# Who makes the low parts of block 2's weights: 42 subtractions move from the vector engine to GpSimd

## The chip, the cores and the metric

The kernel runs on one core of one Trainium2 chip. The metric is the device time of one execution in microseconds (us). The engines are named as the profile names them: PE (TensorE, matmuls), DVE (VectorE), ACT (ScalarE), POOL (GpSimd) and SP (the queue that issues most DMAs). SBUF is the memory on which all engines work, PSUM the small one into which PE writes.

## The reference

Two transformer blocks of two layers each run over 512 tokens of width 1024, all in float32. The change lies in the mixer of block 2, which is called once a layer, so twice in an execution:

```python
def hybrid_mixer(h, positions, w_in, ...):
    (cq, k_att, v_att, k_idx, w_idx,
     q_m, k_m, v_m, o_m, i_m, f_m) = jnp.split(h @ w_in, split_pts, axis=-1)
    cq = rms_norm_2(cq, q_latent_norm)
    q = rope((cq @ w_q_up)...); q_idx = rope((cq @ w_qidx_up)...); k = rope(k_att...)
    att = dsa_attention(q, k, v, q_idx, k_idx, w_idx)      # 256 keys a query, chosen by an indexer
    qk = jax.nn.silu(causal_dwconv(jnp.concatenate([q_m, k_m], -1), conv_w, conv_b))
    hm = mlstm_chunkwise(...)                              # four heads of 128
    hm = jax.nn.sigmoid(o_m) * rms_norm_2(hm, mlstm_out_norm)
    return jnp.concatenate([att, hm], axis=-1) @ w_out
```

The indexer takes relu(q_idx k_idx) of eight heads, weighs them with w_idx, and keeps the best 256 keys of each query.

## The kernel before

**Weights in two parts.** PE multiplies in fp32r, a shortened float32. To keep the precision, every weight and most activations are held as a high part (the value cast to fp32r) and a low part (the value minus the high part), and each product is three matmuls: high by high, high by low, low by high. `wu` (L190) fetches one unit of weights, 128 x 1024 float32 (512 KB): it takes a buffer of the pool `wraw` (three buffers), issues the DMA on SP's queue, and calls `split` (L269). `split` casts on ACT (L273, tile `whi`) and subtracts on DVE (L274, tile `wlo`), or, where a scale is given, L276 and L277. `whi` and `wlo` come from `wpool`, three buffers each, and for the units beyond the third of a common first group from a further pool `wx`. A unit's `wraw` buffer is free for the next DMA when both have read it; `whi` and `wlo` are free when PE has read them.

**What sets the order.** The kernel is written with tiles, and a scheduler at build time sets the order on each engine from its own costs and priorities; each engine then runs its list strictly in order, waiting at an instruction whose input is not there. `wu` runs with a raised priority, so that weights are made as soon as a buffer is free. `split` also serves activations (`qh`, `kidx`, `cqn`, `vm`, `wl`), always on ACT and DVE.

**The stage.** `mixers2` (L1289) is the mixer of block 2. A pass of it has these parts:
- The entry. `gemm_first` runs the products of the first four units (cq in two units, a unit of small columns, the first conv unit), first for tokens 0 to 255, then for 256 to 511, into the banks S, S, o and mm. Meanwhile the second half of the tokens is still being finished: the sum of squares `ss_lat` (L314), a PE matmul that sums it over partitions into T, the reciprocal root (`rsqrt`, L284 to L296, ten tiny DVE instructions), its spread over the rows by PE (L84), the scaling (L1859 in the first pass; L1670 and L1671 in the second), squares and a second `rsqrt`, and the norm (L366 DVE, L367 ACT, L368 DVE), which writes the second half of `h_lat`.
- Conv units 2 to 8 (L1337), mLSTM values (`vunits`), the indexer's up-projection and its rotation (`rope2`, L1263), and the indexer's scores: PE writes S, ACT takes the relu into a tile `g` (L1423), DVE adds it into `work` (L1427).
- The four mLSTM heads (L1456 on), among which the selection of keys (`topk`, MAX8 and MATCH_REPLACE8, L1284 and L1285) runs on DVE, and gate units (`gate`) and the first attention key (`akey`).
- From L1553 on: the values and the attention, where the changed flag is off again.

POOL has almost nothing to do in the stage: one memset of a tile `R` (L1404) a pass.

Of the kernel before, what the change touches and what calls it, by code (L numbers as in the profile page):

```python
# [14 lines left out]
ALU = mybir.AluOpType  # L15
# [24 lines left out]
def f32(ap):  # L40
    return ap.bitcast(F32)
# [45 lines left out]
class Kern:  # L87
# [20 lines left out]
    def load(self, pool, shape, src, dt=F32):  # L108
        x = self.til(pool, shape, dt, self.name("ld"))
        self.nc.sync.dma_start(x, src)  # L110
        return x

    def til(self, pool, shape, dt=F32, tag="t"):
        return pool.tile(shape, dt, tag=tag, name=self.name(tag))

# [78 lines left out]
    def wu(self, src, n=UNIT, scale=1.0, pool=None, at=None):  # L194

        raw = self.til(self.wraw, [P, UNIT], F32, "wraw")
        hi, lo = at or [self.til(pool or self.wpool, [P, UNIT], F32R, x) for x in ("whi", "wlo")]
        with self.tc.high_priority(offset=self.ahead):
            self.nc.sync.dma_start(raw[:, :n], src)
            self.split(hi[:, :n], lo[:, :n], raw[:, :n], scale)  # L200
        return hi, lo

    def raw(self, src, n=UNIT):
# [62 lines left out]
        s, o = lambda: self.bank(self.psS, "S"), lambda: self.bank(self.pso, "o")  # L266
        return [s, s, o] + [self.mmbank] * 3

    def split(self, hi, lo, ps, scale=1.0):  # L269

        nc = self.nc
        if scale == 1.0:
            nc.scalar.copy(hi, ps)  # L273
            nc.vector.tensor_tensor(lo, ps, f32(hi), op=ALU.subtract)  # L274
        else:
            nc.scalar.mul(hi, ps, scale)  # L276
            nc.vector.scalar_tensor_tensor(lo, ps, scale, f32(hi), ALU.mult, ALU.subtract)  # L277
# [1011 lines left out]
    def mixers2(self, l, st, h, gw, cont):  # L1289
        nc, t = self.nc, self.t  # L1290
        V, A = nc.vector, nc.scalar
        c2 = self.c2[:, l]
        wB = t[f"wB{l}"]
        nat = lambda hh, k, i: hh[:, k, i * P:(i + 1) * P]
        es, me, ae = ExitStack(), ExitStack(), ExitStack()
        pool = self.pools(es, "right")
# [113 lines left out]
        for p in range(4):  # L1410
            q = iq[p]
            for b in range(1, 4):
                n = P * (b + 1)
# [43 lines left out]
        for hd in range(4):  # L1457
# [14 lines left out]
            for j in range(4):  # L1472
                n = T - P * j
                ac = acol[:, 4 * j + hd:4 * j + hd + 1]
                ps = self.bank(self.psS, "S")
# [74 lines left out]
        me.close()  # L1550


        yp = self.pools(self.ye)("y", 1)  # L1553
        apool = self.pools(ae)
        av, self.pb, self.pp, self.st = apool("av", 1), apool("pb2", 3), apool("pt2", 2), apool("st2", 4)
        v = self.til(av, [P, 4, 512], F32, "v")
        for hf in range(2):
            units = [self.wu(wB[23 + 2 * hf + i]) for i in range(2)]
            self.nat_gemm(units, h, [lambda a, k, i=i: nat(a, k, i) for i in range(4)], 256,
                          lambda i, ps, hf=hf: A.copy(v[:, i, 256 * hf:256 * hf + 256], ps[:, :256]))  # L1560
# [574 lines left out]
```

## Time and profile before

| | |
|---|---|
| median of 3 runs | 3315.34 us (3312.81 to 3317.41) |
| the profiled execution | 3314.26 us, of which the span from first to last instruction is 3312.5 us |
| PE busy | 3177.1 us, 96% |
| DVE busy | 2017.0 us, 61% |
| ACT busy | 1358.1 us, 41% |
| POOL busy | 66.1 us, 2% |
| DVE, all `wlo<-wraw,whi` at L274 | 484 instructions, 567.5 us |
| first pass of the stage | about 1844 to 2037 us |
| second pass of the stage | about 2574 to 2771 us |

Busy shares are means over the span. In the stage itself the picture differs from part to part, so what matters is read in windows of it: how busy PE and DVE are there, what PE waits for, and at which granted clock PE runs (PEclk, a share of 2.4 GHz; 0.50 is the lower of its two levels, 1.2 GHz).

### The profile page before, as it was taken

The numbers are of one execution on the slowest core, as the hardware profiler recorded it, in microseconds if no ns is written. First come the engines' busy times: TensorE is split into PE (matmuls) and PEld (weight loads), VectorE is DVE, ScalarE is ACT, GpSimd is POOL, SyncE is SP. The second block draws the span as 40 slices with busy tenths as digits, with TensorE's granted clock in tenths as the row PEclk, the third lists the DMA queues.
The fourth block names the chain that finished last, engine by engine and source line by source line (L and its number), as shares of the span: only waits on it lengthen the run. The fifth ranks groups of instructions, "written<-read, shape, count | busy, mean of one in ns | idle before, by whom it ended". The sixth has DMA issues, their size and how long they took to land. (4 is left out here: it accounts for less than half of the span.)

```text
span 3312.5 us, 52585 instructions
## 1 busy us (share of the span) xinstructions
PE 3177.1 (96%) x20884; PEld 2698.2 (81%) x20884; DVE 2017.0 (61%) x4147; ACT 1358.1 (41%) x2405; POOL 66.1 (2%) x91
## 2 busy tenths in 40 slices
PE   7899999999999899989999999989999999999999
PEld 5787778888889877778889968778889868788889
DVE  4757657544345756576665798575656797563335
ACT  4454444212122543443223475543325474543334
POOL 0000001000000001010000000000000000000000
PEclk8899999999999999999999999989999999999999
DMA  7543213324243422125655312244645212232235
GB/s 263 166 160 98 72 51 102 111 94 135 72 137 115 134 71 74 50 90 186 198 183 164 118 45 75 73 160 162 203 162 177 95 51 71 74 112 96 96 116 161
DMA packets 140765, 395.32 MB, mean 119 GB/s; under 512 B 29284, under 2 KB 39268, under 8 KB 140520
## 3 DMA queue, kind: packets, MB, share of 16 engines
q1 hardware_dynamic: 137448, 387.77, 36.1%
q10 hardware_dynamic: 3072, 4.20, 0.5%
q8 instruction: 164, 2.69, 0.3%
q14 instruction: 81, 0.66, 0.1%
HBM read 385.61 MB, written 2.10 MB: 117 GB/s over the span
## 5 line engine op out<-in xcount | busy, mean ns | idle before, releaser
L274 DVE TENSOR_TENSOR wlo<-wraw,whi 128x1024 fp32r<-128x1024 f32 (+3 forms) x484 | 567.5, 1176 | 660.3 <-PE mm L81 389.8
L81 PE MATMUL mm<-h_lat,whi 128*128 128x512 f32 (+1 forms) x3888 | 943.9, 388 | 2.5 <-ACT whi L273 0.9
L81 PEld LDWEIGHTS mm<-h_lat,whi 128*128 128x128 f32 x3888 | 720.1, 189 | 161.4 <-issue 14.0
L273 ACT CAST whi<-wraw 128x1024 fp32r<-128x1024 f32 (+3 forms) x484 | 488.3, 1013 | 849.6 <-PE mm L81 732.1
L81 PE MATMUL mm<-h_lat,wlo 128*128 128x512 f32 (+1 forms) x1944 | 494.3, 385 | 0.0
L81 PEld LDWEIGHTS mm<-h_lat,wlo 128*128 128x128 f32 x1944 | 362.9, 188 | 73.1 <-issue 3.8
L449 DVE SCALAR_TENSOR_TENSOR macc<-mraw,cst,macc 128x512 f32<-128x512 f32 x280 | 207.3, 750 | 37.5 <-DMA mraw<-wm 33.2
L81 PE MATMUL mm<-ah,whi 128*128 128x256 f32 (+1 forms) x702 | 217.7, 310 | 4.1 <-ACT hc L367 4.1
L81 PE MATMUL mm<-al,whi 128*128 128x256 f32 (+1 forms) x702 | 217.5, 310 | 0.0
L81 PE MATMUL mm<-ah,wlo 128*128 128x256 f32 (+1 forms) x702 | 217.5, 310 | 0.0
L81 PE MATMUL mm<-b,whi 128*128 128x256 f32 (+1 forms) x924 | 182.0, 295 | 0.0
L506 ACT ACTIVATE sb<-sb,least 128x512 f32<-128x512 f32 (+4 forms) x184 | 119.0, 647 | 109.9 <-DVE least L503 99.8
L81 PEld LDWEIGHTS mm<-b,whi 128*128 128x128 f32 x924 | 145.4, 188 | 6.0
L81 PEld LDWEIGHTS mm<-ah,whi 128*128 128x128 f32 x702 | 133.0, 189 | 11.7 <-ACT hc L367 4.2
L81 PEld LDWEIGHTS mm<-ah,wlo 128*128 128x128 f32 x702 | 132.8, 189 | 8.1
L81 PEld LDWEIGHTS mm<-al,whi 128*128 128x128 f32 x702 | 133.3, 190 | 7.4
L81 PE MATMUL mm<-b,wlo 128*128 128x256 f32 (+1 forms) x462 | 136.2, 295 | 0.0
L273 ACT CAST ah<-fx 128x256 fp32r<-128x256 f32 (+1 forms) x77 | 43.0, 559 | 200.2 <-DVE fx L1152 200.2
L81 PE MATMUL mm<-whi,h_lat 128*128 128x256 f32 x640 | 117.8, 285 | 2.2 <-DVE vm L274 1.5
L81 PE MATMUL S<-hc,whi 128*128 128x256 f32 (+1 forms) x768 | 107.8, 284 | 3.9 <-ACT whi L273 3.9
L81 PEld LDWEIGHTS mm<-whi,h_lat 128*128 128x128 f32 x640 | 99.9, 191 | 7.2 <-DVE vm L274 2.0
L81 PEld LDWEIGHTS S<-hc,whi 128*128 128x128 f32 (+1 forms) x768 | 97.5, 187 | 6.8 <-ACT whi L273 5.0
(376 smaller groups left out, 5215.2 us busy)
## 6 DMA issues: line engine op xcount, KB each, us to landing
mraw<-wm SPq DMA_DIRECT2D x144, 512.0 KB
wraw<-wgu SPq DMA_DIRECT2D x88, 512.0 KB
wraw<-wgub SPq DMA_DIRECT2D x88, 512.0 KB
wraw<-wA SPq DMA_DIRECT2D x78, 512.0 KB
wraw<-wB SPq DMA_DIRECT2D x54, 512.0 KB
wraw<-wdb SPq DMA_DIRECT2D x56, 448.0 KB
wraw<-wm SPq DMA_DIRECT2D x48, 512.0 KB
wraw<-wd SPq DMA_DIRECT2D x44, 448.0 KB
```

The costliest lines, as they stand in the source:

```text
L81: return self.tell(self.K.nc.tensor.matmul(*a, **k))
L273: nc.scalar.copy(hi, ps)
L274: nc.vector.tensor_tensor(lo, ps, f32(hi), op=ALU.subtract)
L449: V.scalar_tensor_tensor(acc[v], raw[:, i * 512:(i + 1) * 512], c, acc[v], ALU.mult, ALU.add)
L506: A.activation(x["sb"], x["sb"], AF.Exp, bias=x["init"], scale=-1.0, accum_out=x["sum"])
```

## The change

A flag `low_gp` on the kernel object says which engine subtracts in `wu` when no scale is given. It is set at the start of `mixers2` and cleared after its mLSTM part.

```diff
+    low_gp = False
+
@@ def wu
-            self.split(hi[:, :n], lo[:, :n], raw[:, :n], scale)
+            self.split(hi[:, :n], lo[:, :n], raw[:, :n], scale, self.low_gp)
...
-    def split(self, hi, lo, ps, scale=1.0):
+    def split(self, hi, lo, ps, scale=1.0, gp=False):
...
-            nc.vector.tensor_tensor(lo, ps, f32(hi), op=ALU.subtract)
+            (nc.gpsimd if gp else nc.vector).tensor_tensor(lo, ps, f32(hi), op=ALU.subtract)
...
@@ def mixers2
         wB = t[f"wB{l}"]
+        self.low_gp = True
...
         me.close()
...
+        self.low_gp = False
         yp = self.pools(self.ye)("y", 1)
```

It reaches 21 units a pass: four of the entry, seven conv units, four of the mLSTM values, the indexer's up-projection, four gates and the first attention key. The scaled unit (`wqu`, L1528) stays on DVE, and so do all units outside. The number of instructions is unchanged; the scheduler, which sees another engine, also places other instructions anew. In the changed kernel the lines after the flag's definition are two higher, those of `mixers2` three, those behind it four.

DVE at the entry of the first pass, before: the four subtractions stand among the chain of the second half (the fourth, `wlo_18804`, a little further on).

```order
L314 TENSOR_TENSOR ss_lat_84<-ss_lat_84,sq_18563 128x256
L274 TENSOR_TENSOR wlo_18786<-wraw_18784,whi_18785 128x1024
L274 TENSOR_TENSOR wlo_18792<-wraw_18790,whi_18791 128x1024
L1838 SCALAR_TENSOR_TENSOR x_lat<-mm_18566,mod_119,x_lat 128x256
L274 TENSOR_TENSOR wlo_18798<-wraw_18796,whi_18797 128x1024
L314 TENSOR_TENSOR ss_lat_84<-ss_lat_84,sq_18652 128x256
L284 TENSOR_SCALAR rsx_18658<-T_18655 128x2
L287 TENSOR_SCALAR rsy_18659<-rsx_18658 128x2
```

Now, the same place on DVE:

```order
L316 TENSOR_TENSOR ss_lat_84<-ss_lat_84,sq_18563 128x256
L1842 SCALAR_TENSOR_TENSOR x_lat<-mm_18566,mod_119,x_lat 128x256
L316 TENSOR_TENSOR ss_lat_84<-ss_lat_84,sq_18652 128x256
L286 TENSOR_SCALAR rsx_18658<-T_18655 128x2
L289 TENSOR_SCALAR rsy_18659<-rsx_18658 128x2
```

The chain is left alone on DVE, and the subtractions stand on POOL.

PE at the same place, before (S_18808, S_18809 and o_18810 are the banks of the first three units, T_18655 the sum over partitions):

```order
L81 MATMUL S_18809<-h_lat_86,whi_18791 128x256
L81 MATMUL o_18810<-h_lat_85,wlo_18798 128x256
L81 MATMUL o_18810<-h_lat_85,whi_18797 128x256
L81 MATMUL o_18810<-h_lat_86,whi_18797 128x256
L81 MATMUL T_18655<-inv_d,ss_lat_84 128x1 x2
L81 MATMUL o_18810<-h_lat_85,wlo_18798 128x256
```

Now, on PE:

```order
L81 MATMUL S_18808<-h_lat_85,whi_18785 128x256
L81 MATMUL T_18655<-inv_d,ss_lat_84 128x1 x2
L81 MATMUL S_18808<-h_lat_86,whi_18785 128x256
L81 MATMUL S_18808<-h_lat_85,wlo_18786 128x256
L81 MATMUL o_18810<-h_lat_85,wlo_18798 128x256
L81 MATMUL o_18810<-h_lat_85,whi_18797 128x256
```

The sum stood behind the first use of the third unit's low part, and now stands ahead of it, seven matmuls earlier.

POOL from the end of the first pass to the second: nothing stood here before but the memset of `R`. The last rows of the first pass, then the four units of the second pass's entry:

```order
L276 TENSOR_TENSOR wlo_20533<-wraw_20531,whi_20532 128x1024
L276 TENSOR_TENSOR wlo_20574<-wraw_20572,whi_20573 128x1024
L276 TENSOR_TENSOR wlo_25692<-wraw_25690,whi_25691 128x1024
L276 TENSOR_TENSOR wlo_25698<-wraw_25696,whi_25697 128x1024
L276 TENSOR_TENSOR wlo_25710<-wraw_25708,whi_25709 128x1024
L276 TENSOR_TENSOR wlo_25704<-wraw_25702,whi_25703 128x1024
L276 TENSOR_TENSOR wlo_25948<-wraw_25946,whi_25947 128x1024
L1407 MEMSET R_26263 128x512
```

In the second pass the fourth unit (25710) has been placed ahead of the third (25704); ACT's casts stand in that order too, where before the third came first. The memset of `R` stands behind five subtractions.

## Rows read from the trace of the kernel before

**Rows 1.** Windows: stretch, length, busy PE, PEld, DVE, ACT, POOL, PEclk, DMA share, GB/s.

```profile
1843.00:1878.00 35.00, 34.48 (x285) 33.50 (x283) 20.40 (x53) 12.30 (x23) 0.00 (x0) 1.00 0.23 79
...
1950.00:2037.00 87.00, 84.15 (x434) 64.22 (x434) 84.47 (x211) 58.93 (x97) 0.00 (x0) 1.00 0.18 59
```

**Rows 2.** What PE waited for, 1843 to 2037: us in total, times, longest.

```profile
PE S L81 <- DVE w L1483: 1.1, 1, 1.1
PE mm L81 <- DVE vm L274: 0.7, 1, 0.7
PE mm L81 <- DVE g L1343: 0.4, 1, 0.4
...
PE S L81 <- ACT h_lat L367: 0.2, 1, 0.2
```

**Rows 3.** DVE's low parts, 1844 to 2037: count, busy, mean ns, idle before.

```profile
L274 DVE TENSOR_TENSOR wlo<-wraw,whi 128x1024 fp32r<-128x1024 f32 x23 | 27.9, 1220 | 12.1 <-ACT whi L273 10.8 <-ACT wh L273 0.4 <-ACT w L1482 0.4
```

**Rows 4.** POOL's groups over the whole span, the columns of rows 3.

```profile
L784 POOL MEMSET at<- 128x512 f32 x8 | 3.8, 527 | 814.2 <-PE mm L81 611.1 <-DVE yl L274 203.1
L784 POOL MEMSET at<- 128x256 f32 x4 | 1.1, 312 | 0.3 <-POOLq L2126 0.3
```

**Rows 5.** Timeline, POOL and DVE at once: start, length, instruction, idle before.

```profile
328.16 0.73 POOL L1130 TENSOR_TENSOR bias<-bias,rpb 128x256 f32<-128x256 f32 x1 [0.18 <-DMA bias<-nmask]
...
328.04 0.17 DVE L288 TENSOR_TENSOR rsa<-rsy 128x8 f32<-128x8 f32 x1
328.24 0.67 DVE L289 TENSOR_TENSOR rsa<-rsa,rsx 128x8 f32<-128x8 f32 x1
```

**Rows 6.** Timeline, POOL and DVE at a second such place.

```profile
529.80 0.99 POOL L314 TENSOR_TENSOR ss_lat<-ss_lat,sq 128x256 f32<-128x256 f32 x1 [1.97 <-ACT sq L309]
...
529.72 0.48 DVE L368 SCALAR_TENSOR_TENSOR h_lat<-ny,mod,h_lat 128x256 fp32r<-128x256 f32 x1
530.12 0.96 DVE L368 SCALAR_TENSOR_TENSOR hc<-ny,mod,hc 128x256 fp32r<-128x256 f32 x1
```

**Rows 7.** Timeline, entry of the first pass, DVE, and ACT's last square there.

```profile
1844.93 1.23 DVE L274 TENSOR_TENSOR wlo<-wraw,whi 128x1024 fp32r<-128x1024 f32 x1 [0.49 <-ACT whi L273]
1847.37 1.23 DVE L274 TENSOR_TENSOR wlo<-wraw,whi 128x1024 fp32r<-128x1024 f32 x1 [1.22 <-ACT whi L273]
...
1850.13 1.23 DVE L274 TENSOR_TENSOR wlo<-wraw,whi 128x1024 fp32r<-128x1024 f32 x1 [0.47 <-ACT whi L273]
1851.27 0.42 DVE L314 TENSOR_TENSOR ss_lat<-ss_lat,sq 128x256 f32<-128x256 f32 x1
...
1861.66 1.23 DVE L274 TENSOR_TENSOR wlo<-wraw,whi 128x1024 fp32r<-128x1024 f32 x1 [3.46 <-ACT whi L273]
...
1863.19 0.17 DVE L287 TENSOR_SCALAR rsy<-rsx 128x2 int32<-128x2 int32 x1
...
1850.00 0.41 ACT L309 ACTIVATE sq<-x_lat 128x256 f32<-128x256 f32 x1
```

**Rows 8.** Timeline, entry of the second pass: ACT, DVE and PE.

```profile
2579.86 1.05 ACT L273 CAST whi<-wraw 128x1024 fp32r<-128x1024 f32 x1 [0.45 <-DMA wraw<-wB]
...
2582.08 0.42 DVE L314 TENSOR_TENSOR ss_lat<-ss_lat,sq 128x256 f32<-128x256 f32 x1
...
2583.59 0.17 DVE L287 TENSOR_SCALAR rsy<-rsx 128x2 int32<-128x2 int32 x1
...
2597.26 0.41 PE L84 MATMUL T<-ident,rsy 128*128 128x128 f32 x2 [2.12 <-DVE rsy L296]
2598.77 0.58 PE L81 MATMUL S<-h_lat,whi 128*128 128x256 f32 x1 [1.11 <-ACT h_lat L367]
```

**Rows 9.** DVE's adds of the indexer's scores, 1895 to 1950, columns of rows 3.

```profile
L1427 DVE SCALAR_TENSOR_TENSOR work<-g,wcol,work 128x256 f32<-128x256 f32 (+2 forms) x21 | 12.1, 605 | 3.6 <-ACT g L1423 3.4
```

**Rows 10.** Windows with a lowered clock, columns of rows 1.

```profile
1929.80:1935.40 5.60, 5.60 (x14) 4.43 (x14) 5.18 (x10) 2.65 (x6) 0.00 (x0) 0.50 0.01 4
2598.80:2604.40 5.60, 5.60 (x26) 5.60 (x27) 5.04 (x13) 2.77 (x7) 0.00 (x0) 0.50 0.01 3
```

## The prediction

> **What bounds the kernel now.** I read the windows of the stage first. PE is busy for 34.5 of 35 us at the entry of the first pass and for 84.2 of 87 in the mLSTM part, and DVE for 84.5 of those 87 [rows 1]. The reader is to see that PE sets the pace, and that DVE, though full, holds it up little. The list of PE's waits says how little: 1.1 us for `w`, 0.7 for `vm`, 0.4 for `g`, together 2.2 us a pass [rows 2], and none of the list's seven lines names a low part of a weight. So relieving DVE can win only waits of that size, and the question is what the move costs. It can cost at the entries, where the chain of the second half of the tokens ends last: in the first pass PE runs out of first-half products just as the chain ends (a wait of 0.2 us for `h_lat`, rows 2), and in the second it waits 2.12 and 1.11 us for it [rows 8]. What is late on the chain there is late at the end.
>
> **One subtraction.** DVE takes 1.22 us for one [rows 3] (23 rows, of which two are value units, which stay). 21 a pass leave DVE, 25.6 us. POOL's price for this form is in no row. The nearest is the same operation on a quarter of the size, 0.73 us [rows 5]: four of them, 2.9 us, are the upper end, since the fixed part would be paid once. A memset of 128x512 takes 527 ns and of 128x256 312 ns [rows 4], which leaves 0.1 us for the fixed part; 4 x 0.63 + 0.1 = 2.6 us, which I take. The lower end is two memsets of 128x512, 1.05 us, which read nothing.
>
> The Trainium skill has a price for a two-input add of 2048 float32 columns on GpSimd, 4.5 us (GPSIMD Engine Reference, Performance versus the Vector engine); an estimate of half of it is 2.25 us, and the two entries would then come to 4.1 us where I put 5.5 below. No run here shows that size.
>
> **What POOL does to DVE.** While POOL ran 328.16 to 328.89, DVE's L288 took 0.17 us, and L289, which came to the engine at 328.24, took 0.67 and ended just after POOL [rows 5]: it stood until POOL was through. At 529.80 POOL took 0.99 us instead of 0.73, since a DVE instruction was under way, and the next L368 took 0.96 instead of 0.48 [rows 6]. All those DVE instructions read two tensors in SBUF. So the two engines take turns, and whoever comes second waits for the whole of the other. A move of 1.22 us off DVE thus puts up to 2.6 us of standing on it, wherever its next instruction is of that kind. L314, L1427 and the split of activations read two SBUF tensors; products from PSUM (L1343, L366, L1483) and the selection's MAX8 don't.
>
> L287 reads one tensor, and whether it stands too no row above shows. By the Trainium skill (SBUF, State Buffer, Who interferes with whom) it does, since a tensor_scalar within SBUF uses both of DVE's read ports. If it did not, L288 behind it, which reads `rsy` twice, would stand instead, and the sum would be less by 0.2 us.
>
> **Entry of the first pass.** The first subtraction starts at 1844.93 as now and ends at 1847.53; the second follows to 1850.13, the third to 1852.73 (its cast was ready at 1850.13, rows 7). ACT's last square ends at 1850.41 [rows 7], so L314 comes while the third is under way and starts at 1852.73, not at 1851.27: +1.46 us. Behind it on DVE is the whole `rsqrt`; behind the sum on PE, which now stands ahead of the third unit's low part, all first-half products. The fourth cast stands among the squares that this chain releases, so its subtraction moves from 1861.66 to 1863.12 and holds the port to 1865.72. L287 of the second `rsqrt`, 1863.19 + 1.46 = 1864.65, stands to 1865.72: +1.07. Together +2.5 us. With 1.05 us a subtraction the same steps give -0.1, with 2.94 us +2.9.
>
> **Entry of the second pass.** The fourth unit now comes third. Its cast waits for its DMA and ends at 2580.91 [rows 8], so its subtraction runs 2580.91 to 2583.51; the third unit's cast ends at 2581.9 behind it. L314 follows the square at about 2582.5, stands to 2583.5 and ends at 2583.93 (now 2582.50). The third unit's subtraction takes the port to 2586.53. L287 starts 1.09 after the end of L314 now, at 2583.59 [rows 8]; so it would start at 2585.02, but stands to 2586.53: +2.9 us. Ends: +1.0 with 1.05 us, +3.6 with 2.94. PE stands about 1.6 us longer for the fourth cast, which its waits for the chain already cover.
>
> **The rest of a pass.** Four more subtractions follow the entry at once, six lie in the rotation and the indexer, seven in the mLSTM part. PE uses those low parts late enough that 1.4 us more in the making is covered (none is in its list of waits now). A `wraw` buffer is freed when POOL has read it; since POOL's queue is short the SP queue's next DMA waits no longer than 1.4 us more, behind three buffers. The memset of `R` behind five subtractions has until the end of the heads. What is left is the trade on DVE. In the indexer's part 21 adds of 605 ns [rows 9] and the splits read two SBUF tensors, so a subtraction costs DVE nearly its 2.6 us and returns 1.22: 6 x 1.4 = 8.4 us more DVE work, of which 3.4 us go into the idle time ahead of those adds [rows 9], and at worst 5 us reach PE through full `g` tiles, relus and S banks. In the mLSTM part most DVE time is the selection and PSUM products, so a subtraction costs about what it returns. At best all three waits of rows 2 go, -2.2 us. I take +1.0 us a pass, between -2.2 and +5.0: nearer to nothing, as PE has other products to run there.
>
> **Sum.** 2.5 + 2.9 + 2 x 1.0 = +7.4 us. The profiled execution took 3314.26 us (its span 3312.5 and 1.8 around it), so 3321.7; it lay 1.1 us under the median of the runs, 3315.34, so 3322.7 us, +0.22%. Own range: -0.1 + 1.0 - 4.4 = -3.5 us, or 3311.8, and 2.9 + 3.6 + 10.0 = +16.5 us, or 3331.8.
>
> **Rivals.**
> *Covered.* POOL is as quick as its lower end, or the chain finds gaps, and the middle pays for itself: -0.1 + 1.0 = +0.9, 3316.2 us. For it: PE has 190 us of work a pass and little depends on DVE. Against it: 2.9 us stand nearer in kind than two memsets.
> *Faster.* DVE, 25.6 us lighter, is in time everywhere: PE's waits for it go (-4.4), and with them the stretch at half clock that follows a row of waits in the indexer of each pass, 5.6 us at 0.50 [rows 10], which at full clock takes 2.8 (-5.6): -10.0, 3305.3 us. For it: DVE is full at 97% in the mLSTM part. Against it: the stands of rows 5 and 6, and that the scheduler's new order counts on a DVE that is freed. It decides if POOL's instructions hold up DVE by less than 1.2 us each.
> *Slower by more.* The indexer's adds fall behind by the full 5 us a pass, and the new standing at the first entry lowers the clock as the waits of the second do now (5.6 us at 0.50, rows 10: 2.8 us): 5.4 + 10.0 + 2.8 = +18.2, 3333.5 us. For it: PE's order, set without the stands, moves scores ahead of conv products. Against it: rows 2 show waits of 1.1 us that left the clock at 1.00.
>
> **Chances.** Forecast 0.50, covered 0.21, faster 0.10, slower by more 0.19. The predicted time is the forecast's, 3323 us. A measurement of this kernel can tell about 0.2%, 6.6 us, from no change; slower begins at 3322.0, in the middle of the forecast, of which I count 0.28 as slower and 0.22 as the same. Slower 0.28 + 0.19 = 0.47, the same 0.22 + 0.21 = 0.43, faster 0.10. The range is 3309 to 3334: the forecast's own, widened up to the slow rival and down by a part of the fast one.
>
> **What would show it.** POOL's 42 rows of `wlo` at a mean of 2.4 to 3.0 us, some longer where DVE was first. At both entries L316 and L289 with several times their usual length, ending with a POOL row, and PE waiting for `T` or `h_lat` by 2 to 3 us more than now. In the indexer single adds of 2 to 3 us. DVE's busy time in a pass would fall by much less than 25.6 us. Wrong would be: POOL rows under 1.5 us; two-tensor DVE instructions of normal length beside them; low parts in PE's list of waits past the entries; or a time that comes from stages outside the two passes.

## The result, and the profile after

The changed kernel takes 3330.51 us (median of nine runs, 3324.10 to 3343.24), the kernel before 3311.84 us (nine runs, 3307.18 to 3317.41): ratio 1.0055, 95% interval 1.0044 to 1.0065, so 18 us slower (15 to 22). The profiled execution of the changed kernel took 3324.68 us with a span of 3322.9 us, 10.4 us more than that of before. This one lies 5.8 us under the median of its kernel and the profiled one of before 2.4 us over that of its own, so the two traces show only part of the 18 us.

To see where the time went, the same instructions are looked for in both traces. Timeline of the kernel before at three places of each pass (DVE's first sum of squares at the entry; PE spreading the second reciprocal root; PE's longest wait of the attention; the second place of the second pass stands in [rows 8]):

```profile
1839.31 0.42 DVE L314 TENSOR_TENSOR ss_lat<-ss_lat,sq 128x256 f32<-128x256 f32 x1
1865.08 0.40 PE L84 MATMUL T<-ident,rsy 128*128 128x128 f32 x2 [0.22 <-DVE rsy L296]
2076.56 0.49 PE L81 MATMUL S<-qh,qh 64*128 64x128 f32 x4 [1.91 <-DVE qh L1273]
...
2571.23 0.42 DVE L314 TENSOR_TENSOR ss_lat<-ss_lat,sq 128x256 f32<-128x256 f32 x1
...
2810.98 0.49 PE L81 MATMUL S<-qh,qh 64*128 64x128 f32 x4 [2.03 <-DVE qh L1273]
```

The same places of the changed kernel:

```profile
1837.61 0.42 DVE L316 TENSOR_TENSOR ss_lat<-ss_lat,sq 128x256 f32<-128x256 f32 x1
1866.25 0.40 PE L84 MATMUL T<-ident,rsy 128*128 128x128 f32 x2 [0.18 <-DVE rsy L298]
2081.38 0.52 PE L81 MATMUL S<-qh,qh 64*128 64x128 f32 x4 [1.91 <-DVE qh L1275]
...
2573.29 0.42 DVE L316 TENSOR_TENSOR ss_lat<-ss_lat,sq 128x256 f32<-128x256 f32 x1
...
2602.65 0.40 PE L84 MATMUL T<-ident,rsy 128*128 128x128 f32 x2 [1.66 <-DVE rsy L298]
...
2818.88 0.72 PE L81 MATMUL S<-qh,qh 64*128 64x128 f32 x4 [2.03 <-DVE qh L1275]
```

From place to place the entry of the first pass takes 28.64 us instead of 25.77 (+2.9), the rest of that pass 215.13 instead of 211.48 (+3.7), the entry of the second 29.36 instead of 26.03 (+3.3), the rest 216.23 instead of 213.72 (+2.5). Together +12.4 us; all stages outside gave 2.0 us back.

Windows of the changed kernel, first the entry and then the mLSTM part of the first pass (they answer to [rows 1]: stretch, length, busy PE, PEld, DVE, ACT, POOL, PEclk, DMA share, GB/s), and behind them POOL's group of subtractions (count, busy, mean ns, idle before):

```profile
1843.00:1878.00 35.00, 32.76 (x259) 31.88 (x259) 16.19 (x46) 10.41 (x21) 9.57 (x4) 0.95 0.24 76
1950.00:2037.00 87.00, 83.25 (x415) 62.23 (x414) 84.21 (x207) 58.72 (x95) 16.66 (x7) 0.98 0.19 61
```

```profile
L276 POOL TENSOR_TENSOR wlo<-wraw,whi 128x1024 fp32r<-128x1024 f32 x42 | 104.4, 2496 | 1177.1 <-ACT whi L275 1060.0 <-PE mm L81 75.7 <-ACT g L1426 22.2
```

PE is busy 1.7 us less at the entry, and DVE, in the mLSTM part, is as full as before (84.2 of 87 us) although seven subtractions have left it. From the first to the third place the lengths of DVE's rows add up to 206.7 us, where they made 219.7: 13 us less, for the 25.6 us of work that went. (A row overlaps the next a little; busy time, which counts such overlaps once, fell from 196.1 to 186.7 us.) In the other 12.6 us DVE stood behind POOL: by as much its rows are longer than rows of the same form before. Standing counts as busy. Timeline of the changed kernel at the first entry, POOL, DVE and PE (it answers to [rows 7]), then at the second ([rows 8]):

```profile
1848.47 2.37 POOL L276 TENSOR_TENSOR wlo<-wraw,whi 128x1024 fp32r<-128x1024 f32 x1 [0.36 <-ACT whi L275]
1862.08 2.41 POOL L276 TENSOR_TENSOR wlo<-wraw,whi 128x1024 fp32r<-128x1024 f32 x1 [11.24 <-ACT whi L275]
...
1848.74 2.38 DVE L316 TENSOR_TENSOR ss_lat<-ss_lat,sq 128x256 f32<-128x256 f32 x1 [0.80 <-ACT sq L311]
...
1864.27 0.25 DVE L289 TENSOR_SCALAR rsy<-rsx 128x2 int32<-128x2 int32 x1
...
1851.27 0.58 PE L81 MATMUL T<-inv_d,ss_lat 128*128 128x1 f32 x4 [1.64 <-DVE ss_lat L316]
...
2583.37 4.90 POOL L276 TENSOR_TENSOR wlo<-wraw,whi 128x1024 fp32r<-128x1024 f32 x2 [2.08 <-ACT whi L275]
...
2584.92 1.14 DVE L316 TENSOR_TENSOR ss_lat<-ss_lat,sq 128x256 f32<-128x256 f32 x1 [8.89 <-ACT sq L311]
...
2587.84 0.45 DVE L289 TENSOR_SCALAR rsy<-rsx 128x2 int32<-128x2 int32 x1
```

The add L316, 0.42 us by itself, shows 2.38 and 1.14 us, and each time ends 0.3 us behind an instruction of POOL (at 1850.84, and at 2585.77, the first of the two in that row); PE, which had no such wait before, stands 1.64 us for it. The same happens in the heads, here with the low part of `w`, which takes 0.55 us where nothing is in its way:

```profile
1973.66 2.39 POOL L276 TENSOR_TENSOR wlo<-wraw,whi 128x1024 fp32r<-128x1024 f32 x1 [4.79 <-ACT g L1347]
...
1974.01 0.41 DVE L1287 MATCH_REPLACE8 work<-m,work 128x256 f32<-128x256 f32 x1
1974.34 2.13 DVE L276 TENSOR_TENSOR wl<-w,wh 128x384 fp32r<-128x384 f32 x1
...
1976.52 0.45 PE L81 MATMUL o<-wl,vm 128*128 128x384 f32 x1 [1.35 <-DVE wl L276]
```

The selection's instruction ran beside POOL at its usual 0.41 us; the two-tensor split stood, and PE with it. PE's waits of the first pass up to the attention, in the changed kernel (they answer to [rows 2]: us in total, times, longest):

```profile
PE o L81 <- DVE wl L276: 2.0, 2, 1.4
PE T L81 <- DVE ss_lat L316: 1.6, 1, 1.6
PE S L81 <- ACT g L1426: 1.2, 5, 0.4
PE mm L81 <- DVE vm L276: 0.7, 1, 0.7
PE T L84 <- DVE den L1524: 0.6, 1, 0.6
...
PE S L81 <- DVE w L1486: 0.4, 1, 0.4
```

Of the waits that could be won, `w` fell from 1.1 to 0.4 (in the second pass it is 1.2) and that of L1343 went; `vm` stayed. In their place stand `wl`, `ss_lat` and `den`, 4.2 us.

### The profile page after: what moved, and what is told of

It is laid out like the page before. It is cut to its first block, busy times and chain, and to the rows that moved or that the text cites. A ratio compares the mean times of both kernels' runs of the same rounds, so it can differ in the third digit from the quotient of the medians.

```text
span 3322.9 us, 52608 instructions
## 1 busy us (share of the span) xinstructions
PE 3179.9 (96%) x20884; PEld 2695.8 (81%) x20884; DVE 1997.0 (60%) x4105; ACT 1360.5 (41%) x2405; POOL 168.9 (5%) x133
## 5 line engine op out<-in xcount | busy, mean ns | idle before, releaser
L276 DVE TENSOR_TENSOR wlo<-wraw,whi 128x1024 fp32r<-128x1024 f32 (+3 forms) x442 | 517.2, 1173 | 645.5 <-PE mm L81 390.5
L81 PEld LDWEIGHTS mm<-h_lat,whi 128*128 128x128 f32 x3888 | 716.6, 189 | 159.7 <-issue 12.6
L276 POOL TENSOR_TENSOR wlo<-wraw,whi 128x1024 fp32r<-128x1024 f32 x42 | 104.4, 2496 | 1177.1 <-ACT whi L275 1060.0
L81 PEld LDWEIGHTS mm<-ah,whi 128*128 128x128 f32 x702 | 132.7, 189 | 11.8 <-ACT hc L369 4.2
L81 PE MATMUL S<-h_lat,whi 128*128 128x256 f32 (+1 forms) x448 | 96.7, 303 | 9.0 <-ACT h_lat L369 5.1
```

The costliest lines, as they stand in the source:

```text
L81: return self.tell(self.K.nc.tensor.matmul(*a, **k))
L276: (nc.gpsimd if gp else nc.vector).tensor_tensor(lo, ps, f32(hi), op=ALU.subtract)
```

## The experiments

The theory is the lock: a subtraction on POOL and a DVE instruction that takes two tensors from SBUF do not run at once, DVE stands, and PE behind it. The rivals: PE waits for POOL's low parts because they are made more slowly; the scheduler's new order costs; and, for the size, PE's clock. The table gives the time against the kernel before (ratio with its interval), and by the trace the lengths between the places above, less those of before, in us.

| kernel | ratio | entry 1 | rest 1 | entry 2 | rest 2 |
|---|---|---|---|---|---|
| changed, first trace | 1.0055 (1.0044 to 1.0065) | +2.9 | +3.7 | +3.3 | +2.5 |
| changed, again | 1.0055 (1.0039 to 1.0071) | +1.9 | +8.7 | +3.3 | +2.8 |
| entries on DVE | 1.0041 (1.0025 to 1.0057) | 0.0 | +3.6 | -0.5 | +3.2 |
| entries alone on POOL | 1.0024 (1.0015 to 1.0032) | +2.0 | +0.1 | +4.6 | -2.1 |
| in quarters | 1.0055 (1.0041 to 1.0068) | +1.8 | +6.0 | +6.1 | +1.4 |
| no low part | 0.9977 (0.9967 to 0.9986) | -0.1 | -4.9 | -0.5 | -5.4 |
| POOL's work added | 1.0153 (1.0140 to 1.0167) | +7.0 | +17.6 | +6.9 | +16.6 |
| heads alone | 1.0107 (1.0093 to 1.0122) | 0.0 | +17.3 | +0.4 | +18.5 |
| middle alone | 1.0012 (1.0003 to 1.0021) | 0.0 | -0.5 | -0.5 | 0.0 |
| heads less two units | 1.0064 (1.0052 to 1.0076) | 0.0 | +9.0 | +0.1 | +9.0 |
| heads in quarters | 1.0019 (1.0010 to 1.0027) | 0.0 | +1.0 | -0.2 | +3.7 |
| last five units alone | 0.9996 (0.9986 to 1.0006) | 0.0 | -0.7 | +0.1 | -2.5 |

**The changed kernel again.** No edit.

> The changed kernel once more, for its spread and its clock. In the profiled run the two passes cost +5.5 and +5.8 us against the kernel before, about +11 us in all, though the median of nine runs was +18.7 us with granted clocks from 0.978 to 0.984. Theory 'lock' (GpSimd's subtractions hold up VectorE, which holds up TensorE at the entries and at the mLSTM heads): the same stands in the same places, +9 to +12 us by the trace where the clock is 0.983. Rival 'clock' (the greater part is stretches at half clock that the new waits bring on): where the mean clock is 0.978, the trace shows several stretches at 0.50 in or behind the two passes that the first trace did not have, each worth 1.7 to 3.4 us, and the sum is +20 us or more.

Its trace shows the same waits at the entry and nearly the same in the heads, and the rest of the first pass is 5.0 us longer than in the first trace. The windows of the indexer at the same instructions, the first trace of the changed kernel and then this one:

```profile
1919.00:1946.00 27.00, 25.81 (x111) 15.50 (x110) 24.46 (x44) 19.20 (x37) 4.27 (x2) 1.00 0.12 39
```

```profile
1923.50:1950.50 27.00, 26.25 (x90) 15.39 (x88) 21.67 (x33) 15.93 (x31) 2.99 (x2) 0.75 0.11 39
```

PE's waits there are 1.2 us in the first and 0.7 in the second, but in the second the granted clock is 0.75 over 27 us, that is 13.6 us at its lower level: (1 - 0.75) x 27 = 6.8 us lost. The first trace lost 1.7 us further on (0.98 of the 87 us of the mLSTM part), so the clock makes 5.1 us of difference, which is all of it. The rival "clock" holds for this pass, and the lock for the places where PE stands. Which of the two clocks a run gets, the waits listed do not decide. In all, the passes of this trace are 16.8 us longer than before, between what the two theories gave (+9 to +12, +20 or more), and another 6.6 us lie outside the passes.

**Entries on DVE.**

```diff
         wB = t[f"wB{l}"]
-        self.low_gp = True
...
         we.close()
+        self.low_gp = True
         mpool = self.pools(me)
```

> The four units of each entry are again subtracted on VectorE; the other 17 a pass stay on GpSimd. Lock: the entries come back to their lengths of before (no wait for ss_lat, L287/L289 at 0.17 us), which takes off 2.9 us in the first and 3.3 in the second pass, so about 6 us less than the changed kernel, +4 to +6 us against the kernel before by the trace. Rival 'order' (what costs is the scheduler's new order of TensorE and VectorE, not the standing): the order at the entries comes back too, but the rest of the pass is placed anew and the gain is not tied to the entries. Rival 'late low parts' (TensorE waits for GpSimd's slower subtraction itself): takes off only the waits for GpSimd's wlo at the entries, 0.4 us in the first and 1.1 in the second pass.

Both entries are back at their lengths of before, and the sum by the trace is +6.3 instead of +12.4 us, as the lock expected; the rest keeps its +3.6 and +3.2. The ratio, 1.0041 (+13.6 us), lies lower than the changed kernel's, but the intervals overlap.

**Entries alone on POOL.**

```diff
         we.close()
+        self.low_gp = False
         mpool = self.pools(me)
...
-        self.low_gp = False
         yp = self.pools(self.ye)("y", 1)
```

> Only the four units of each entry are subtracted on GpSimd, the other 17 a pass on VectorE as before. Lock: +2.9 us in the first and +3.3 us in the second pass, about +6 us (+0.19%) against the kernel before, and nothing in the rest of the passes. Order: the middle parts move as well. If the entries' cost were paid back later, the kernel would be within 2 us of the kernel before.

+7.9 us (5.0 to 10.6), and by the trace +2.0 and +4.6, with 2.1 us given back in the rest of the second pass, where 6.8 us run at half clock instead of 13.6. The rest of the first pass did not move. So the entries cost by themselves about what was expected of them. In the second entry it is not the lock alone: PE waits 2.4 us there for POOL's low parts, against 1.0 in the whole change.

**In quarters.**

```diff
-            (nc.gpsimd if gp else nc.vector).tensor_tensor(lo, ps, f32(hi), op=ALU.subtract)
+            if gp:
+                for c in range(0, UNIT, 256):
+                    x = slice(c, c + 256)
+                    nc.gpsimd.tensor_tensor(lo[:, x], ps[:, x], f32(hi[:, x]), op=ALU.subtract)
+            else:
+                nc.vector.tensor_tensor(lo, ps, f32(hi), op=ALU.subtract)
```

> All 21 units a pass on GpSimd, but each subtraction in four instructions of 128x256 instead of one of 128x1024. Lock: VectorE can come in after each quarter, so it stands at most about 0.7 us at a time instead of up to 2.4; the wait for ss_lat in the first entry falls from 1.6 us to under 0.5, the stands of L289 and L276 (wl, qh) to 0.7 or less, and the kernel comes out 3 to 8 us better than the changed one. Late low parts: the four instructions together take 2.6 to 2.9 us instead of 2.4, the low parts come later, and the kernel is 1 to 3 us worse than the changed one. Order: the same as the changed kernel within 2 us.

No gain and no loss. In number that is what the rival "order" expected, and neither of the other two did; but by the trace two effects cancel. The stands became shorter, DVE's add at the first entry among them, and from the last score of the indexer to the attention the passes take 2.3 and 3.8 us more than before, instead of 5.9 and 5.6. At the entries PE now waits for POOL itself. Timeline of DVE at the first entry, and PE's waits at the second:

```profile
1852.07 1.04 DVE L321 TENSOR_TENSOR ss_lat<-ss_lat,sq 128x256 f32<-128x256 f32 x1 [0.80 <-ACT sq L316]
...
1854.47 0.65 DVE L295 TENSOR_TENSOR rsa<-rsy 128x2 f32<-128x2 f32 x1
```

```profile
PE mm L81 <- ACT whi L275: 2.2, 1, 2.2
PE o L81 <- POOL wlo L279: 1.7, 1, 1.7
PE T L84 <- DVE rsy L303: 1.7, 1, 1.7
```

The add (L316 of the changed kernel, L321 here) shows 1.04 instead of 2.38 us, yet two of the ten tiny instructions of the root stand behind the next quarter (0.35 instead of 0.17 us, and 0.65 instead of 0.16). At the second entry the low part comes too late by 1.7 us, where one piece was late by 0.7. At the entries, then, lateness is a part of the price, and cutting trades one for the other.

**No low part.**

```diff
-        hi, lo = at or [self.til(pool or self.wpool, [P, UNIT], F32R, x) for x in ("whi", "wlo")]
+        one = self.low_gp and scale == 1.0
+        hi, lo = at or [self.til(pool or self.wpool, [P, UNIT], F32R, x) for x in (("whi",) if one else ("whi", "wlo"))] + [None] * one
...
-            self.split(hi[:, :n], lo[:, :n], raw[:, :n], scale, self.low_gp)
+            if one:
+                self.nc.scalar.copy(hi[:, :n], raw[:, :n])
+                lo = hi
+            else:
+                self.split(hi[:, :n], lo[:, :n], raw[:, :n], scale)
```

> The relief alone: in the 21 units a pass the low part is left out, and TensorE multiplies by the high part in its place (so the output's precision is lost there, the work of TensorE is the same). VectorE loses 25.6 us a pass as in the change, and GpSimd does nothing. Theory 'lock, and nothing to win': TensorE's waits for w, vm and g of the kernel before, 2.2 us a pass, go at best, so between -1 and -7 us against the kernel before. Rival 'the relief is worth much, the lock eats it': -10 us or more, by as much as the stretches at half clock in the indexer go too. Rival 'order' (the new order by itself costs): no gain or a loss although nothing stands.

-7.6 us (4.6 to 10.9). That is what DVE's relief is worth here when it costs nothing. The interval holds both the end of what the lock theory allowed (-7) and the rival's -10, and the rival's reason shows in the trace: in the two passes the time at half clock is 3.4 us, where the trace of before has 20.4, so part of the gain may be clock. PE's waits of the first pass have shrunk to five lines, of which the first two are:

```profile
PE mm L81 <- DVE vm L281: 0.7, 1, 0.7
PE T L84 <- DVE den L1529: 0.7, 1, 0.7
```

**POOL's work added.**

```diff
-            (nc.gpsimd if gp else nc.vector).tensor_tensor(lo, ps, f32(hi), op=ALU.subtract)
+            nc.vector.tensor_tensor(lo, ps, f32(hi), op=ALU.subtract)
+            if gp:
+                nc.gpsimd.tensor_tensor(ps, ps, f32(hi), op=ALU.subtract)
```

> The lock alone: VectorE makes all low parts as before, and GpSimd runs a subtraction of the same form behind it, into the buffer of the raw weights, which nobody reads. No low part is late and VectorE is not relieved. Lock: VectorE's instructions with two SBUF inputs stand as in the changed kernel (up to 2.4 us), now without 25.6 us a pass given back; at least as slow as the changed kernel, +12 to +30 us. Late low parts: TensorE waits for none of GpSimd's results, so within 3 us of the kernel before (a weight buffer is freed 2.4 us later, which three buffers should cover).

+51 us, more than either expected, and no low part of PE's comes from POOL. PE's first waits of the first pass:

```profile
PE S L81 <- ACT g L1428: 4.0, 4, 2.0
PE T L81 <- issue: 2.8, 1, 2.8
PE o L81 <- DVE wl L276: 2.7, 3, 1.2
PE S L81 <- DVE w L1488: 2.4, 2, 1.3
```

With the work of before left on DVE, 21 idle subtractions on POOL cost 24 us a pass, in all four parts of the table. Nobody reads what POOL makes here, PE waits for no DMA, and the other engines keep their order nearly whole: from the end of the first entry to the attention 1136 of PE's 1140 rows and 387 of DVE's 393 come as before, by their names. So the lock is dear without any late result of POOL's and without a new order. It is not the price of the lock in the change: DVE's own low parts stand too here (some 7 us a pass more than before), and 47.6 us of the two passes run at half clock, where the trace of before has 20.4.

**Heads alone**, and **middle alone.** The flag is set ahead of the loop over the heads; or set behind `we.close()` and cleared ahead of that loop.

```diff
-        self.low_gp = True
...
+        self.low_gp = True
         for hd in range(4):
```

> Only the 11 units a pass that are made during the four mLSTM heads (conv units, values, gates, the key) are subtracted on GpSimd. Lock: the split of w (wl, L276) stands up to 2.1 us as in the changed kernel and TensorE waits for it 1.4 + 0.7 us, while its waits for w, g and vm of before partly go: +1 to +4 us a pass, +2 to +8 us in all. Relief: here VectorE is 97% busy, so if the move pays anywhere it is here: -2 to -5 us.

> Only the six units a pass between the entry and the heads (conv and values of the first heads, the indexer's up-projection) on GpSimd. Lock: L1277 and the splits of qh stand 1 to 1.8 us four times a pass, of which little reaches TensorE: 0 to +2.5 us a pass. With the 11 units of the heads alone and the four of the entries alone the parts should sum to the changed kernel, +11 us by the trace within about 3 us. The indexer's stretch at half clock (6.8 us in the kernel before; 10.2 and 3.4, or none, in the kernels with these units on GpSimd) is expected to differ from the kernel before here and not in the kernel with the heads alone.

The middle costs little (+4.0 us, 1.0 to 6.9; nothing by the trace, in which 6.8 us less than before run at half clock). The heads alone cost +35 us, twice the whole change: both theories missed it, and the parts do not sum (entries +4.7, middle -0.9, heads +36 by the trace, the whole +12.4). Timeline of the kernel with the heads alone at the last rotation of the indexer, POOL, DVE, PE; then the window that follows:

```profile
1913.78 2.39 POOL L276 TENSOR_TENSOR wlo<-wraw,whi 128x1024 fp32r<-128x1024 f32 x1 [4.43 <-PE mm L81]
1913.84 2.88 DVE L1277 TENSOR_TENSOR g<-g,g 128x512 f32<-128x512 f32 x1
...
1919.63 1.33 PE L81 MATMUL S<-kidx,qh 64*128 64x384 f32 x3 [2.59 <-ACT g L1425]
```

```profile
1919.60:1943.20 23.60, 22.88 (x62) 13.48 (x63) 16.19 (x28) 11.44 (x21) 2.57 (x1) 0.50 0.06 22
```

One stand of 2.2 us (L1277, 0.69 us where nothing is in its way) lies where PE has nothing left to run, behind one of 1.4 us of `qh`; PE waits 2.59 us, and behind that wait the clock is 0.50 for 23.6 us, up to 11.8 us lost, where the kernel before loses up to 3.4; the second pass repeats it. In the whole change the same two subtractions meet the same rotations and `qh` shows 2.0 and 2.5 us, but six units have left DVE ahead of them: taken from the entry's end, PE's first scores that had to wait start 2.0 us earlier than here (1919.66 - 1866.25 = 53.41 us, against 1919.63 - 1864.25 = 55.38), and PE waits 0.4 us.

Why the parts do not sum can be narrowed with the granted clocks of all runs. One minus the mean clock, times the span, is the most that the lower clock can have cost: 58 to 60 us in the kernel before, 62 in the changed one, 63 with the entries alone, 60 with the middle alone, but 85 with the heads alone. What is left without it grows by 5, 2 and 8 us in the three parts, 14 together, and by 17 in the whole. If all of that time was lost, the parts sum to within 3 us, and it is the clock that does not. This is an estimate, and all of it is the upper bound: among the runs of one kernel, a microsecond counted so goes with only some 0.6 us of time.

**Heads less two units**, and **heads in quarters.** Of the 11 units of the heads the first two stay on DVE; or all 11 go to POOL, each in the four pieces shown above.

```diff
-        self.low_gp = True
...
         for hd in range(4):
+            if hd == 1:
+                self.low_gp = True
```

> As the kernel with the 11 units of the heads on GpSimd (+1.07%), but the first two of them, the conv units whose subtraction lay in the last rotations of the indexer, stay on VectorE; nine a pass on GpSimd. Theory 'one stand and the clock': there qh stood 2.1 us and L1277 2.9 us behind GpSimd, TensorE waited 2.6 us for g, and the clock fell to 0.50 for 23.9 us in each pass. Without the two the wait is 0.7 us as in the kernel before, the long stretches are gone (12 us each), and the kernel is within -2 to +8 us of the kernel before. Rival 'order of the heads' (the loss comes from the other nine, or from TensorE's new order): still +20 us or more.

> The 11 units of the heads on GpSimd, each subtraction in four instructions of 128x256; the order on the other engines is nearly that of the kernel in one piece. Lock: qh and L1277 stand 0.7 us at most at a time, so the wait of 2.6 us for g in the indexer falls to about 1 us or less and with it the 23.9 us at half clock; 15 to 35 us better than in one piece, between 0 and +15 us against the kernel before. If order or lateness made the loss, it stays at +30 us or more.

Without the two units the wait of 2.6 us for `g` and the 23.6 us at half clock are gone, 8 to 10 us a pass. But 9 us a pass remain, and +21 us in all (17 to 25), where -2 to +8 was expected: by its number the rival "order of the heads" was met. These 9 us lie behind the last score, in the heads: PE's waits there are 4.0 us longer in each pass, and 10.2 and 6.8 us run at half clock, where the trace of before has none. The first of PE's waits of the first pass in that kernel, and behind them those of the heads in quarters:

```profile
PE S L81 <- DVE w L1487: 1.7, 3, 1.1
PE o L81 <- DVE wl L276: 1.6, 1, 1.6
PE o L81 <- ACT wh L275: 1.3, 2, 1.0
PE T L84 <- DVE den L1525: 1.2, 1, 1.2
PE mm L81 <- DVE g L1345: 1.2, 1, 1.2
```

```profile
PE S L81 <- DVE w L1491: 1.1, 1, 1.1
PE S L81 <- ACT g L1430: 1.0, 2, 0.7
PE o L81 <- DVE wl L281: 0.9, 2, 0.6
```

So the loss of the heads has two halves: the stands of `qh` and L1277 in the indexer with the clock behind them, and in the heads the waits for `w`, `wl` and L1345, with more time at half clock. Cutting the subtraction takes away most of both: +6.3 us (3.3 to 8.9) instead of +35, with the same engine, the same units and the same bytes. The order is the same too: from the end of the first entry to the attention all rows of DVE and ACT and all but one of PE's 1140 come in the same order in both kernels, by their names. So the order did not make the loss. Lateness did not either: in no kernel with the entries on DVE does one of PE's waits name a low part of POOL's. The length of one turn is what costs here.

**Last five units alone.** As above with `hd == 3`: four gates and the first key.

> Only the last five units a pass, four gates and the first key, on GpSimd; they lie behind the indexer, where VectorE is at its fullest and no chain of TensorE ends. If any part of the change pays, this one: -3 to +1 us. Lock without a chance to pay: the split of w stands 1 to 1.8 us four times a pass and TensorE waits for it, +1 to +4 us a pass.

-1.3 us (-4.6 to +2.0): not to be told from the kernel before. PE waits for `den` 0.9 us, which it did not, and its waits for `w` stay at 1.2. By the trace the passes are 0.7 and 2.5 us shorter than before, but ahead of the five units, where less time is at half clock; behind the last score they are 0.9 and 0.7 us longer. No version was found that is faster than the kernel before beyond doubt.

## Why the prediction held, and where it was short

**Direction and range.** Slower by more than 0.2% had the largest chance (0.47), and 3330.5 us lies in 3309 to 3334. The forecast itself, +7.4 us, is 5 us short of the stages' 12.4 and 11 us short of the medians' 18. In absolute terms it missed by less, since the nine runs of before have a median 3.5 us under that of the three that were known. Taken as a difference, 18 us lies outside the forecast's own range (-3.5 to +16.5); that the time lies under the upper end of that range, 3331.8, is the luck of the lower median. The range also holds a slip: with 2.94 us a subtraction the steps of the first entry end at +3.9 (the third subtraction at 1853.75, the fourth at 1867.08, less 1863.19), not +2.9, which puts its upper end at +17.5. And the stretches at half clock of [rows 10] last 6.8 us each; the 5.6 us of the rivals are the length of the window.

**One subtraction.** Taken at 2.6 us between 1.05 and 2.9: it takes 2.35 to 2.43 where nothing is in its way. The estimate from the Trainium skill (GPSIMD Engine Reference, Performance versus the Vector engine), 2.25 us, was the nearer one, 0.15 us short.

**Taking turns.** As [rows 5, 6] showed it. L287, of which no row said whether it stands, does: it shows 0.25 and 0.45 us instead of 0.17, as L289 of the changed kernel, ending with a POOL row (1864.49 and 2588.27). The Trainium skill (SBUF — State Buffer, Who interferes with whom) counts tensor_scalar among the operations that can contend with GpSimd. The trace agrees.

**First entry, +2.5 forecast, +2.9 measured.** The add ends 1.13 us later in the pass than before (forecast 1.46). The second stand was 0.08 us instead of 1.07, as L289 came 2.2 us behind the start of the fourth subtraction, where the steps have 1.5. In its place the clock fell to 0.50 for 3.4 us behind PE's wait of 1.64 us, which loses up to 1.7 us; the second trace lacks that stretch and shows +1.9, 0.9 less. Here the sum was nearly right with one term wrong and one missing.

**Second entry, +2.9 forecast, +3.3 measured.** By the steps: the add ends 1.50 us later in the pass (forecast 1.43), and L289 behind its stand ends 2.5 us later (forecast 2.9). PE's wait for the fourth cast, put at 1.6 us and covered, is 1.3 us and covered. What the steps left out is a wait of 0.7 us for POOL's low part, behind the sum.

**The rest, +1.0 a pass forecast, +3.7 (8.7 in the second trace) and +2.5 measured.** This is the term that was too small. The step that failed is "in the mLSTM part most DVE time is the selection and PSUM products, so a subtraction costs about what it returns". The shares were right, and MAX8 and MATCH_REPLACE8 do run beside POOL; but what PE waits for in the heads goes through the few instructions that don't, L1482 (of the changed kernel, which makes `w`) and the split of `w`. A share of DVE's time was used where the question was which instructions lie on the chain. From the last score to the attention the passes are 5.9 and 5.6 us longer. Some 2.6 us of each are twelve matmuls that the new order has placed behind the last score instead of ahead of it; the other 3.3 and 3.0 are the price of the heads, of which PE's waits make 1.5 and 2.2, and 3.4 us at half clock in the first pass up to 1.7. Between the entry's end and the last score the changed kernel differs by no more than half a microsecond once these matmuls are counted there. But 0 and 3.4 us run at half clock there, where the trace of before has 6.8 and 13.6, so the stands of the indexer may cost 3 to 5 us a pass that these lengths do not show; that stays open.

That DVE gets back 1.22 us for each 2.4 was right in kind: without a price the relief wins 7.6 us; POOL's 42 turns without the relief cost 51; the change pays some 18, less than the two together, since with POOL's work added DVE's own low parts stand too. Of the signs named, single adds of 2 to 3 us in the indexer did not come (none is over 0.75 us); `qh` and L1277 stood instead, and the adds only in other kernels.

**The clock** stood only in the rivals. It belongs in the range more than in the sum: the two traces of the changed kernel differ by 5 us in the rest of the first pass, with no larger waits in the indexer, where the clock fell, and in the two passes together they have 13.6 and 23.8 us at half clock, the trace of before 20.4. Over all runs it is at most some 3 of the 18 us. Of the rivals, slower by more named the size (+18.2), the indexer and the half clock; but what it put on the adds of the scores was paid in the heads, and its full mechanism came only with the heads alone. What decides between the two clocks stays open.

**Order.** The placing of instructions anew is not the cause by itself: with POOL's work added the order is nearly that of before, and the kernel is 51 us slower; the heads in one piece and in quarters have one order, and differ by 29 us; without low parts the order is new as well, and the kernel is faster; with the entries alone the rest keeps its length to 0.1 us in the first pass. That the heads cost more alone than within the whole goes with the clock; that the clock falls there and not in the whole may come from the 2 us of lead that the rotation has in the whole, which was read from the traces and not tried apart.

## What to carry to other kernels

Before work goes to GpSimd from a full VectorE, list which VectorE instructions in that stage read two SBUF tensors and lie on the chain that TensorE waits for: each will stand for up to the whole length of a GpSimd instruction, whatever the mean load says. Where the result has slack, cut the GpSimd instruction into pieces; four pieces took 29 of 35 us off here, much of it time at the lower clock, and won nothing at the entries, where the result was needed at once. Price a wait of TensorE with what its clock does behind it, not by its own length.

## What the runs showed of the hardware

The turns bind GpSimd too. Timeline of POOL in the indexer of the changed kernel, and of DVE there:

```profile
1930.48 3.91 POOL L276 TENSOR_TENSOR wlo<-wraw,whi 128x1024 fp32r<-128x1024 f32 x1 [11.12 <-ACT g L1426]
...
1929.68 2.45 DVE L1430 SCALAR_TENSOR_TENSOR work<-g,wcol,work 128x384 f32<-128x384 f32 x4
```

Four adds in a row kept their turn, and the subtraction, begun at 1930.48, took 3.91 us instead of 2.4: it got in only when they were through. A wait of TensorE of 2.59 us was followed by 23.6 us at the lower clock, so that it cost up to 14 us; in two executions of one and the same program the same stretch had either no such time or 13.6 us of it.
